# The projection's stores issued on GpSimd's queue instead of SyncE's, in a one-core diffusion-transformer layer

## The chip, the cores and the metric

The kernel runs on one core of one Trainium2 chip. Its time is device microseconds of one execution; the figure shown is the median of several executions. One profiled execution of the same program gives the trace: for every instruction its engine, its start and its length, and for every idle stretch what ended it. Five engines work side by side, each through its own list of instructions, strictly in order: PE multiplies matrices, DVE (VectorE) and ACT (ScalarE) do elementwise work, POOL (GpSimd) too, and SP (SyncE) only issues transfers. A transfer is issued from the list of some engine and then runs on 16 shared DMA engines; an instruction in a list that has to wait for something holds up everything behind it in that list.

## The reference

One layer over 2048 latent tokens and 256 context tokens, width 1024, all in float32.

```python
h     = modulate(x, norm1_g, shift, scale)       # RMSNorm, then (1 + scale) and shift
p     = h @ w_in        # columns: k | v | q | u | vg | gate_attn | gate_gmlp
...
q, k  = rmsnorm(q, q_norm_g), rmsnorm(k, k_norm_g)   # then rotary on both
attn  = attend(q, all latent and context k, v)
gm    = u * (W_s @ norm(vg) + b)                     # in chunks of 128 tokens
y     = sigmoid(gate_attn) * (attn @ w_br_attn) + sigmoid(gate_gmlp) * (gm @ w_br_gm)
x     = x + g1 * (y @ w_out)
x     = x + g2 * (square(relu(modulate(x, norm2_g, ...) @ w_ff1)) @ w_ff2)
```

That is the mathematics in short; heads, blocks and the context's own key and value columns are left out.

## The kernel before

**Stages.** The program runs the projection (until about 750 us), attention, the two branches' merge, and the feed-forward part. Every float32 operand is split into a high and a low half, and every product is three matmuls (L1705, L1706, L1707 for the wide ones; L185 to L187 for small ones). Latent tokens come in four blocks of 512 and are projected in two pairs of blocks. The 1792 columns ahead of the gates form two "pairs" (index 0: keys, values and queries, two halves of 384 columns; index 1: `u` and `vg`, two of 512), and the 2048 gate columns are cut into eight `Gate`s of two times 128 columns, for each pair of blocks. For both, a scheme of Strassen's kind is used: 7 products instead of 8, over sums and differences of the two blocks' halves and of the weights' halves. So the projection's elementwise work has to make weight combinations, operand halves and sums of products, besides the splits.

**What the projection stores.** Six places write intermediate tiles to HBM, where a later step loads them again:

- L556 in `h_ahead`: the second pair of blocks' normalized tokens, turned (16 stores of 256 KB into `h_d`).
- L628 in `opening_terms` and L677 in `terms`: the weights' combinations of pair 0 (16 of 192 KB) and pair 1 (16 of 256 KB), into `t_d`. `pair_chunk` loads them again at L701, ACT splits off the high half at L703 and DVE the low half at L704; then PE can use them. `terms` takes its four tiles of a round from the `m` buffers, of which there are four: two are loaded with weights (L663) and two hold the results (L670 to L673) until the four stores at L677 have landed.
- L2086 in `Pair.leave`: the sums of products of the pairs (64 stores into `pr_d`, shown as `p_d` in the profile). Half of them are issued by ACT, which has just copied them; the other half, which DVE adds up at L2084, by SP.
- L2103 in `Gate.store`: the gates' tanh (64 of 256 KB into `ta_d` and `tb_d`). ACT makes it at L2130 after DVE's sum (L2144 for product 4, L2149 for product 2), or straight from PSUM.
- L825 in `keys_work`: the finished keys (10 stores into `k_d`). Their making starts with statistics over the heads (L771) and ends with DVE's low half at L812 and PE's transposes at L191.

**What sets the order.** The projection is written as interleaved generators: a product's steps (`pairs_run`, `Gate.step`) call `tick`, which advances the queued work (`keys_work`, `queries_work`, `mixing`). Within the projection the compiler's scheduler then places each instruction on its engine's list by its own model of when it would be ready; only some loads, and the walls between stages, are pinned by hand. From attention on, the lists of PE and DVE are fixed by hand. Hence a change of a store's queue can move other instructions on any engine in the projection. The scheduler also hands out completion semaphores: transfers of SP and ACT share eight in turn, those of POOL have eight of their own, and a transfer waits until the one eight places earlier in that turn has landed.

**Buffers.** `t2` has six buffers of 2 KB a partition, `t4` eight of 4 KB, `m` four of 4 KB. A store that lands later keeps its buffer longer.

**POOL** has no work in the projection besides a few constants at the start; its sums for the modulation (L2299) begin when attention does.

Of the kernel before, what the change touches and what calls it, by code (L numbers as in the profile page):

```python
# [18 lines left out]
P = 128  # L19
# [25 lines left out]
HK = KC // 2  # L45
# [5 lines left out]
def f32(ap):  # L51
    return ap.bitcast(F32)
# [19 lines left out]
class Kern:  # L72
# [474 lines left out]
    def h_ahead(self, blk):  # L547
        for i in range(2):
            xs = self.x_load(self.x_block(2 * blk + i), TT, self.m4)
            yield  # L550
            self.h_scale(xs)
            yield
            for k in range(KC):
                ot = self.t2([TB])
                self.turn(xs, k, ot)
                self.nc.sync.dma_start(self.h_d[i][k % HK][:, k // HK], ot)  # L556
                yield

    def operand(self, p, src):
# [36 lines left out]
    def opening_terms(self, pair, direct):  # L596
        nc = self.nc
        tt, sub = nc.vector.tensor_tensor, ALU.subtract
        n, w = pair.n, self.I["w_in"][0]
        b, t = {}, {}  # L600
        for kk in range(HK):
            for k in (kk, kk + HK):
                r = [self.h2([n]) for _ in range(2)]
                for j in range(2):
                    lo = pair.lo + j * n
                    nc.sync.dma_start(r[j], w[k * P : (k + 1) * P, lo : lo + n])
                b[k] = [r[j] for j in pair.cols]
        yield

        def term(p, kk, in0, in1):  # L610
            t[p, kk] = self.sb("hx", [n])
            tt(out=t[p, kk], in0=in0, in1=in1, op=sub)

        def first(kk):
            term(4, kk, b[kk][1], b[kk][0])
            term(5, kk, b[kk + HK][1], t[4, kk])

        def split(p, c):
            hi, lo = self.f4([2, n], F32R), self.f4([2, n], F32R)
            direct.append([(hi[:, s], lo[:, s]) for s in range(2)])  # L620
            for s in range(2):
                nc.scalar.copy(hi[:, s], t[p, 2 * c + s])
            for s in range(2):
                tt(out=lo[:, s], in0=t[p, 2 * c + s], in1=f32(hi[:, s]), op=sub)

        def store(p):
            for kk in range(HK):
                nc.sync.dma_start(self.t_d[pair.index][p][kk // 2][kk % 2], t[p, kk])  # L628

        first(0)  # L630
        yield
        first(1)
        yield
        split(5, 0)
        yield
        first(2)
        first(3)
        yield
        split(5, 1)
        yield  # L640
        for kk in range(HK):
            term(6, kk, b[kk + HK][1], b[kk][1])
        for c in range(2):
            split(6, c)
        store(4)
        yield
        for kk in range(HK):
            term(3, kk, b[kk + HK][0], t[5, kk])
        store(3)
        yield  # L650
        store(6)
        store(5)
        yield

    def terms(self, pair, alloc):
        nc = self.nc
        tt, sub = nc.vector.tensor_tensor, ALU.subtract
        n, w = pair.n, self.I["w_in"][0]
        for kk in range(HK):
            rows = []  # L660
            for k in (kk, kk + HK):
                r = alloc([2, n])
                nc.sync.dma_start(  # L663
                    r.rearrange("p j c -> p (j c)"),
                    w[k * P : (k + 1) * P, pair.lo : pair.lo + 2 * n],
                )
                rows.append([r[:, j] for j in pair.cols])
            (b11, b12), (b21, b22) = rows
            t12, t34 = alloc([2, n]), alloc([2, n])
            tt(out=t12[:, 0], in0=b12, in1=b11, op=sub)  # L670
            tt(out=t12[:, 1], in0=b22, in1=t12[:, 0], op=sub)
            tt(out=t34[:, 0], in0=b22, in1=b12, op=sub)
            tt(out=t34[:, 1], in0=b21, in1=t12[:, 1], op=sub)  # L673
            for p, src in (
                (4, t12[:, 0]), (5, t12[:, 1]), (6, t34[:, 0]), (3, t34[:, 1]),
            ):
                nc.sync.dma_start(self.t_d[pair.index][p][kk // 2][kk % 2], src)  # L677
            yield

    def pair_load(self, pair, p, c):  # L680
# [109 lines left out]
    def keys_work(self, nt, b, kraw=None):  # L790
        nc = self.nc
        c = 0 if b is None else b + 1
        if b is not None:
            kraw = self.t2([TT, NKV, HD])
            nc.sync.dma_start(
                kraw.rearrange("p t h d -> p t (h d)"), self.rows(self.pr_d[0][b][0], slice(0, P))
            )
            yield
            yield
        (rb,) = self.heads_rstd([kraw[:, :nt]], 1.0 / HD)  # L800
        nc.vector.tensor_tensor(out=kraw[:, :nt], in0=kraw[:, :nt], in1=rb, op=ALU.mult)
        yield
        kr = self.t2([TT, NKV, HD])
        if b is None:
            g = self.rg["k"].unsqueeze(1).unsqueeze(1).broadcast_to([P, nt, NKV, HD])
            nc.vector.tensor_tensor(out=kr[:, :nt], in0=kraw[:, :nt], in1=g, op=ALU.mult)
        else:
            self.rope(self.rope_tables("k", b), kraw, kr, self.t2([TT, NKV, HD]), NKV)
        yield
        kk = self.m4([TT, NKV, 2, HD], F32R)  # L810
        nc.scalar.copy(kk[:, :nt, :, 0, :], kr[:, :nt])
        nc.vector.tensor_tensor(  # L812
            out=kk[:, :nt, :, 1, :], in0=kr[:, :nt], in1=f32(kk[:, :nt, :, 0, :]),
            op=ALU.subtract,
        )
        yield
        n = nt * P
        for kv in range(NKV):
            ps = self.bank([TB])
            self.transposes(  # L820
                ps, [f32(kk[:, t, kv]).rearrange("p a d -> p (a d)") for t in range(nt)]
            )
            ka = self.t2([TB])
            nc.scalar.copy(ka[:, :n], ps[:, :n])
            nc.sync.dma_start(self.k_d[c][kv][:, :n], ka[:, :n])  # L825
        yield

    def queries_work(self, b):
# [246 lines left out]
    def project(self, tail):  # L1075
# [9 lines left out]
        direct = []  # L1085
        terms = self.opening_terms(pairs[0], direct)
        next(terms)
        self.loads.append(range(at, self.here()))
        h[0], h[1] = [], []
# [9 lines left out]
        def opening(raw=raw, h=h):  # L1099
# [6 lines left out]
            for c in range(2):  # L1106
                for kk in (2 * c, 2 * c + 1):
                    t = raw[0, kk]
                    self.turn(self.x0, kk + HK, t[:, 1])
                    h[1].append(self.operand(1, t[:, 1]))  # L1110
                ready.append(self.pair_chunk(pairs[0], 1, c, loaded[2 + c]))
                next(terms)
            yield
            turned = self.raw_turned(1, x1, raw, self.t4)
            next(turned)
            next(terms)
            yield
            next(turned)
# [707 lines left out]
    def ff2(self, blk, side):  # L1826
# [60 lines left out]
        def take(p, t):  # L1887
            ps = banks[p][t]
            if p in (0, 5, 6):
                u = u3 if p == 6 else u2  # L1890
                u[t] = self.sb("f2", [TB])
                nc.scalar.copy(u[t], ps)
            else:
                leave(p, t, ps)
                if p == 1:
                    nc.scalar.copy(ps, u2[t])
# [159 lines left out]
class Pair:  # L2056
# [21 lines left out]
    def leave(self, i, j, t, ps, u=None):  # L2078
        k, nc = self.k, self.nc
        x = k.t2([TB])[:, : self.n]  # L2080
        if u is None:
            nc.scalar.copy(x, ps)
        else:
            nc.vector.tensor_tensor(out=x, in0=u, in1=ps, op=ALU.add)  # L2084
        dst = k.pr_d[self.index][2 * self.blk + i][j]
        (nc.scalar if u is None else nc.sync).dma_start(dst[t * P : (t + 1) * P, :], x)  # L2086


class Gate:
# [9 lines left out]
    def store(self, i, j, src):  # L2099
        k = self.k  # L2100
        dst = (k.ta_d, k.tb_d)[self.g // HK][2 * self.blk + i]
        lo = (2 * (self.g % HK) + j) * P
        self.nc.sync.dma_start(dst[lo : lo + P, :], src)  # L2103

    def last_weights(self, load):
        k, nc = self.k, self.nc
# [285 lines left out]
```

## Time and profile before

| what | value |
| --- | --- |
| median of three executions | 3017.25 us (3015.89, 3017.25, 3019.2) |
| profiled execution: whole / span of instructions | 3021.28 / 3019.5 us |
| granted TensorE clock, mean of the span | 0.989 |
| PE busy | 2942.4 us (97%) |
| DVE / ACT / POOL busy | 2091.8 / 1429.2 / 652.7 us |
| transfers | 537.02 MB in 385503 packets |
| reading of HBM / writing | 370.32 / 164.10 MB |

A row of a timeline gives the start, the length, the engine, the line of the program, the operation, and the tiles written and read (numbers of buffers left out); the bracket at the end says how long the engine sat idle before it and what ended that. A row of the view of waits adds up such idle time by what was waited for: engine, line, what released it, then microseconds in all, the number of times, and the longest. `SPq` is SP's list of transfers. The granted clock is the share of full speed that the chip's throttle gave TensorE.

### The profile page before, as it was taken

How to read it: one execution, taken by the hardware profiler on the slowest of the kernel's cores; microseconds unless marked ns; L12 is line 12 of the kernel's file. 1: busy time of each engine (PE TensorE's matmuls, PEld its weight loads, DVE VectorE, ACT ScalarE, POOL GpSimd, SP SyncE). 2: the span in 40 equal slices, each digit the busy share in tenths (PEclk: the TensorE clock that was granted, in tenths of full speed). 3: DMA queues.
4: the chain of work that ended last, by engine and by line, in shares of the span. 5: the costliest groups of instructions: out<-in, count | busy, mean ns of one | idle time of the engine just before them, and what ended most of it. 6: DMA issues, size and time to landing. Idle time of an engine off the chain costs nothing.

```text
span 3019.5 us, 37930 instructions
## 1 busy us (share of the span) xinstructions
PE 2942.4 (97%) x13325; PEld 2216.2 (73%) x13325; DVE 2091.8 (69%) x3019; ACT 1429.2 (47%) x2330; POOL 652.7 (22%) x470
## 2 busy tenths in 40 slices
PE   7899999999999999999999989999999999999999
PEld 5778788875555555555888878888887888888887
DVE  5857577885788888777655588776676766654555
ACT  5545765563455454544222254444454344444432
POOL 0000000000899899985212200000000000000000
PEclk9999999999999999999999999999999999999999
DMA  7586666554000010005766559888766544447554
GB/s 275 183 292 204 209 212 212 194 174 147 28 29 29 29 35 23 19 22 180 248 208 213 170 190 317 306 303 299 264 229 223 186 154 153 151 152 279 209 208 154
DMA packets 385503, 537.02 MB, mean 178 GB/s; under 512 B 37968, under 2 KB 197888, under 8 KB 385312
## 3 DMA queue, kind: packets, MB, share of 16 engines
q1 hardware_dynamic: 372944, 513.87, 51.5%
q10 hardware_dynamic: 12368, 20.73, 1.8%
q8 instruction: 105, 1.72, 0.2%
q14 instruction: 86, 0.70, 0.1%
HBM read 370.32 MB, written 164.10 MB: 177 GB/s over the span
## 4 chain that ended last, share of the span: by engine, by line
PE 84%; DVE 6%; DMA 5%; ACT 3%; issue 2%; SPq 0%; POOL 0%; ACTq 0%; DVEq 0%; POOLq 0%
PE b L1705 14%; PE b L1706 14%; PE b L1707 14%; PE b L2279 9%; PE b L2248 5%; PE b L2267 4%; PE b L185 4%; PE b L186 4%; PE b L187 4%; PE b L2203 3%; PE a L1705 3%; PE a L1706 3%; PE a L1707 3%; PE b L191 1%; DMA m<-in_w_in 1%
## 5 line engine op out<-in xcount | busy, mean ns | idle before, releaser
L2214 DVE TENSOR_REDUCE ts<-b 128x1 f32<-128x512 f32 x512 | 313.2, 683 | 74.7 <-PE b L2203 74.7
L2299 POOL TENSOR_TENSOR ac<-ac,p 128x512 f32<-128x512 f32 x214 | 306.4, 1463 | 51.6 <-ACT p L2271 51.6
L1821 DVE TENSOR_TENSOR b<-b,b 128x1024 fp32r<-128x1024 f32 x170 | 200.8, 1221 | 135.4 <-ACT b L1820 135.1
L1820 ACT CAST b<-b 128x1024 fp32r<-128x1024 f32 x170 | 170.6, 1050 | 223.8 <-PE b L1707 98.8
L2271 ACT ACTIVATE p<-b 128x512 f32<-128x512 f32 x384 | 194.1, 627 | 169.6 <-PE b L2267 168.9
L1706 PE MATMUL b<-b,b 128*128 128x512 f32 x680 | 265.2, 390 | 3.3 <-DVE b L1821 3.3
L1705 PE MATMUL b<-b,b 128*128 128x512 f32 x680 | 266.1, 391 | 1.7 <-DVE f L1842 1.5
L1707 PE MATMUL b<-b,b 128*128 128x512 f32 x680 | 264.7, 389 | 0.0
L2299 POOL TENSOR_TENSOR ac<-p,p 128x512 f32<-128x512 f32 x32 | 52.5, 1658 | 757.1 <-DMA raw<-in_w_mod 752.5
L2299 POOL TENSOR_TENSOR ac<-ac,t 128x512 f32<-128x512 f32 x152 | 204.9, 1376 | 0.0
L2248 PE MATMUL b<-h,h 128*128 128x512 f32 x576 | 189.2, 409 | 3.6 <-ACT p L2271 2.0
L2279 PE MATMUL b<-p,h 128*64 128x512 f32 x768 | 186.4, 608 | 0.0
L2267 PE MATMUL b<-h,h 128*128 128x512 f32 x576 | 179.8, 393 | 0.0
L1706 PE MATMUL b<-hb,b 128*128 128x512 f32 x446 | 173.8, 390 | 0.0
L1715 DVE TENSOR_TENSOR f<-f,b 128x512 f32<-128x512 f32 x160 | 109.3, 683 | 80.3 <-issue 46.6
L1705 PE MATMUL b<-hb,b 128*128 128x512 f32 x415 | 161.8, 390 | 0.0
L1707 PE MATMUL b<-hb,b 128*128 128x512 f32 x415 | 161.2, 389 | 0.0
L2248 PEld LDWEIGHTS b<-h,h 128*128 128x128 f32 x576 | 104.7, 190 | 65.0 <-DVE ts L2214 25.9
L1706 PEld LDWEIGHTS b<-b,b 128*128 128x128 f32 x680 | 127.7, 188 | 31.8 <-DVE b L1821 5.2
L1705 PEld LDWEIGHTS b<-b,b 128*128 128x128 f32 x680 | 127.6, 188 | 29.7 <-ACT b L1820 2.3
L1707 PEld LDWEIGHTS b<-b,b 128*128 128x128 f32 x680 | 127.7, 188 | 26.4
L1718 ACT ACTIVATE f<-f 128x512 f32<-128x512 f32 x96 | 60.5, 630 | 140.8 <-DVE f L1715 140.8
(434 smaller groups left out, 7290.7 us busy)
## 6 DMA issues: line engine op xcount, KB each, us to landing
ao_d<-f SPq DMA_DIRECT2D x224, 256.0 KB
f<-in_w_ff SPq DMA_DIRECT2D x48, 1024.0 KB
b<-ao_d SPq DMA_DIRECT2D x85, 512.0 KB
b<-w2o_d SPq DMA_DIRECT2D x85, 512.0 KB
w2o_d<-f SPq DMA_DIRECT2D x112, 256.0 KB
f<-in_w_in SPq DMA_DIRECT2D x44, 512.0 KB
f<-x_d SPq DMA_DIRECT2D x64, 256.0 KB
hb<-ao_d SPq DMA_DIRECT2D x54, 256.0 KB
```

What stands on the lines that cost most here:

```text
L185: mm(ps, sh, mh, start=start, stop=False)
L1705: mm(ps, wh, hh, start=start and k == 0, stop=False, skip_group_check=True)
L1706: mm(ps, wh, hl, start=False, stop=False, skip_group_check=True)
L1707: mm(ps, wl, hh, start=False, stop=k == len(w) - 1, skip_group_check=True)
L1820: nc.scalar.copy(h, f32(l))
L1821: nc.vector.tensor_tensor(out=l, in0=f32(l), in1=f32(h), op=ALU.subtract)
L2214: nc.vector.tensor_reduce(out=self.mx[:, t, h, c : c + 1], in_=ps[h], axis=AX.X, op=ALU.max)
L2248: self.nc.tensor.matmul(self.pts[j][h], k.KA[c][self.kv][:, ks], self.qa[h], start=True, stop=False, skip_group_check=True,)
L2267: self.nc.tensor.matmul(s, k.KB[c][self.kv][:, ks], self.qb[h], start=False, stop=True, skip_group_check=True,)
L2271: self.nc.scalar.activation(pt[h], s, AF.Exp)
L2279: nc.tensor.matmul(self.o[h * HD : (h + 1) * HD, :], k.V[c][:, i, self.kv * HD : (self.kv + 1) * HD], pt[h], start=j == 0, stop=j == NKT - 1,)
L2299: nc.gpsimd.tensor_tensor(out=self.acc[e][:, h], in0=old[:, h], in1=pt[h], op=ALU.add)
```

## The change

In six places, `nc.sync.dma_start` becomes `nc.gpsimd.dma_start`. What is stored, from where and to where stays the same. ACT's half of the stores of `Pair.leave`, and all loads, stay where they are.

```diff
 h_ahead
-                self.nc.sync.dma_start(self.h_d[i][k % HK][:, k // HK], ot)
+                self.nc.gpsimd.dma_start(self.h_d[i][k % HK][:, k // HK], ot)
...
 opening_terms
-                nc.sync.dma_start(self.t_d[pair.index][p][kk // 2][kk % 2], t[p, kk])
+                nc.gpsimd.dma_start(self.t_d[pair.index][p][kk // 2][kk % 2], t[p, kk])
...
 terms
-                nc.sync.dma_start(self.t_d[pair.index][p][kk // 2][kk % 2], src)
+                nc.gpsimd.dma_start(self.t_d[pair.index][p][kk // 2][kk % 2], src)
...
 keys_work
-            nc.sync.dma_start(self.k_d[c][kv][:, :n], ka[:, :n])
+            nc.gpsimd.dma_start(self.k_d[c][kv][:, :n], ka[:, :n])
...
 Pair.leave
-        (nc.scalar if u is None else nc.sync).dma_start(dst[t * P : (t + 1) * P, :], x)
+        (nc.scalar if u is None else nc.gpsimd).dma_start(dst[t * P : (t + 1) * P, :], x)
...
 Gate.store
-        self.nc.sync.dma_start(dst[lo : lo + P, :], src)
+        self.nc.gpsimd.dma_start(dst[lo : lo + P, :], src)
```

POOL's list grows from 276 rows to 430, SP's shrinks by the same 154. The compiler's scheduler moves other instructions with them. Three pieces of the difference between the two programs' lists follow: a row with a minus stands there before, one with a plus now, one without either in both.

On SP, the rounds in which `terms` makes pair 1's weight combinations beside the first two gates (`ta_d` are the gates' stores, `t_d` the combinations', `m` the weights, `f4` and `e2` other loads):

```order
-L2103 DMA ta_d1_107<-t4_312_1629 128x512
 L663 DMA m_354_1845<-in_w_in 128x1024
 L663 DMA m_355_1847<-in_w_in 128x1024
-L2103 DMA ta_d0_106<-t4_349_1825 128x512
 L685 DMA f4_385_2011<-in_w_in 128x2x512
-L677 DMA t_d512_4_0_177<-m_356_1849 128x512
-L677 DMA t_d512_5_0_179<-m_356_1849 128x512
-L677 DMA t_d512_6_0_181<-m_357_1850 128x512
-L677 DMA t_d512_3_0_175<-m_357_1850 128x512
-L2103 DMA ta_d0_106<-t4_307_1582 128x512
 L663 DMA m_361_1881<-in_w_in 128x1024
 L663 DMA m_362_1883<-in_w_in 128x1024
```

The stores between the rounds' loads have gone to POOL's list, and the loads of the second round follow those of the first with one load between them.

On DVE, the same rounds (the rows of L670 to L673 are a round each; `t4_349` and `t4_342` are a gate's sums, whose products lie in the PSUM bank `b_341`):

```order
 L672 TENSOR_TENSOR m_364_1886<-m_362_1883,m_361_1881 128x512
 L673 TENSOR_TENSOR m_364_1886<-m_362_1883,m_363_1885 128x512
-L2144 TENSOR_TENSOR t4_349_1825<-t4_342_1773,b_341_1760 128x512
-L704 TENSOR_TENSOR f4_395_2082<-f4_394_2080,f4_396_2083 128x1024
-L2149 TENSOR_TENSOR t4_342_1773<-t4_342_1773,b_341_1760 128x512
 L670 TENSOR_TENSOR m_368_1914<-m_366_1910 128x512
 L671 TENSOR_TENSOR m_368_1914<-m_367_1912,m_368_1914 128x512
 L672 TENSOR_TENSOR m_369_1915<-m_367_1912,m_366_1910 128x512
 L673 TENSOR_TENSOR m_369_1915<-m_367_1912,m_368_1914 128x512
-L704 TENSOR_TENSOR f4_408_2141<-f4_408_2141,f4_409_2143 128x1024
+L2144 TENSOR_TENSOR t4_349_1825<-t4_342_1773,b_341_1760 128x512
+L704 TENSOR_TENSOR f4_395_2082<-f4_394_2080,f4_396_2083 128x1024
 L670 TENSOR_TENSOR m_372_1942<-m_370_1938 128x512
+L2149 TENSOR_TENSOR t4_342_1773<-t4_342_1773,b_341_1760 128x512
```

The gate's two sums have moved from ahead of the third round to behind it, the second of them behind the first row of the fourth round too.

On PE, around a small product of the mixing (`b_680`, whose input was loaded shortly before) between wide products of gates (`b_662`):

```order
 L1706 MATMUL b_662_3620<-h_195_1028,f4_654_3574 128x512
 L1707 MATMUL b_662_3620<-h_194_1027,f4_655_3575 128x512
-L1705 MATMUL b_662_3620<-h_196_1031,f4_654_3574 128x512
-L1706 MATMUL b_662_3620<-h_197_1032,f4_654_3574 128x512
-L1707 MATMUL b_662_3620<-h_196_1031,f4_655_3575 128x512
-L1705 MATMUL b_662_3620<-h_198_1035,f4_654_3574 128x512
-L1706 MATMUL b_662_3620<-h_199_1036,f4_654_3574 128x512
-L1707 MATMUL b_662_3620<-h_198_1035,f4_655_3575 128x512
 L185 MATMUL b_680_3715<-m_677_3709,m_679_3713 128x256
 L186 MATMUL b_680_3715<-m_678_3710,m_679_3713 128x256
```

The small product stands six wide matmuls earlier than before.

## The prediction

> **What bounds the kernel now.** I began with the page's busy times and its chain of waits.
>
> ```profile
> PE 2942.4 (97%) x13325; PEld 2216.2 (73%) x13325; DVE 2091.8 (69%) x3019; ACT 1429.2 (47%) x2330; POOL 652.7 (22%) x470
> PE 84%; DVE 6%; DMA 5%; ACT 3%; issue 2%; SPq 0%; POOL 0%; ACTq 0%; DVEq 0%; POOLq 0%
> ```
>
> PE is idle for 77 us of a span of 3019.5, so no scheduling change can bring more than a few tens of microseconds. All 154 moved stores lie in the projection, so next came the windows of 50 us there (columns: elapsed, busy of PE, PEld, DVE, ACT, POOL, then the granted clock, the transfers' share, GB/s).
>
> ```profile
> 50.00:100.00 50.00, 45.65 (x242) 42.47 (x243) 43.12 (x75) 35.00 (x65) 0.00 (x0) 0.93 0.52 169
> 100.00:150.00 50.00, 41.93 (x220) 36.46 (x219) 39.64 (x90) 27.34 (x45) 0.00 (x0) 0.90 0.59 181
> 150.00:200.00 50.00, 45.81 (x204) 36.65 (x203) 28.30 (x49) 19.03 (x32) 0.00 (x0) 0.98 0.86 289
> 200.00:250.00 50.00, 49.51 (x230) 40.44 (x229) 36.08 (x67) 24.21 (x36) 0.00 (x0) 0.99 0.75 248
> 650.00:700.00 50.00, 41.40 (x183) 32.61 (x182) 31.19 (x53) 24.96 (x39) 0.00 (x0) 0.90 0.51 161
> ```
>
> PE's idle time is 4.35, 8.07, 4.19, 0.49 and 8.60 us in these; the two windows with the most also have the lowest clock, 0.90. The transfers are at 0.86 of their engines only from 150 to 200. POOL is empty. What PE waits for between 45 and 750 us, and what SP's list waits for up to 840 us, came last:
>
> ```profile
> PE a L1705 <- ACT a L2150: 8.3, 3, 5.1
> PE b L990 <- ACT m L519: 6.3, 2, 5.7
> PE b L185 <- DMA m<-ws_d: 4.4, 5, 2.4
> PE b L191 <- DVE m L812: 2.9, 1, 2.9
> SPq L2103 <- ACT t L2130: 148.8, 44, 11.3
> SPq L2086 <- DVE t L2084: 43.2, 25, 6.4
> SPq L556 <- ACT t L528: 24.1, 14, 8.7
> SPq L628 <- DVE hx L612: 23.4, 12, 10.0
> ACT f L703 <- DMA f<-t_d: 33.6, 11, 8.3
> ```
>
> SP spends 239.5 us (the four SP rows) at the head of its list on a store whose data isn't ready, with loads behind it. That is a lot, but no store is waited for by PE: PE waits for ACT and DVE. A load that comes earlier counts only where one of these four kinds of wait ends with it.
>
> **What the change removes.** SP's waits above, and the issues:
>
> ```profile
> L677 SPq DMA_DIRECT2D t_d<-m x16: 319/320/423, 159.0 to 192.1; - x16
> ```
>
> A store's issue has a median of 320 ns; 154 of them are 49 us of SP's list over 700 us. None of it is on the chain (SPq 0%), so by itself it is worth nothing. In sentences apart: the Trainium skill's page "DMA: Bandwidth & Descriptors", section "Issuing engines are not separate DMA queues", says that issuing from several engines saves only the sequencer's time, usually little beside the transfer. By that rule alone the sum would be zero; the waits of 239.5 us are the larger saving here, and no run yet shows what they are worth.
>
> **What it adds on POOL.** The trace has no transfer issued by POOL. The nearest rows bound it: SP's 0.32 us below, POOL's own work on such a tile above.
>
> ```profile
> L2299 POOL TENSOR_TENSOR ac<-ac,p 128x512 f32<-128x512 f32 x214 | 306.4, 1463 | 51.6 <-ACT p L2271 51.6
> POOL ac L2299 <- DMA raw<-in_w_mod: 752.5, 1, 752.5
> L2103 SPq DMA_DIRECT2D tb_d<-m x8: 319/322/338, 698.7 to 743.1; - x8
> ```
>
> 154 times 0.32 to 1.46 us is 49 to 225 us, inside the 752.5 us in which POOL has nothing to do, and I take zero for it. If that cover were gone, the last stores of the gates (up to 743.1) would hold back L2299, which has slack until the feed-forward part; a few microseconds at most. What counts is a later landing: a store that lands 1 us later keeps its `m` buffer 1 us longer. In `terms`, a round's results need the buffers of the round before, whose stores are issued 5 us or more ahead of the next L670 (rows below), so up to about 4 us later landing is hidden.
>
> **Where a load comes earlier: the context keys.** The longest gap of PE up to 600 us, and what stands before it, from the timelines of PE, ACT and SP:
>
> ```profile
> 111.00 0.47 PE L990 MATMUL b<-ident,m 128*128 128x128 f32 x1 [5.70 <-ACT m L519]
> 106.64 0.83 ACT L703 CAST f<-f 128x768 fp32r<-128x768 f32 x1 [6.24 <-DMA f<-t_d]
> 96.71 2.25 SPq L2086 DMA_DIRECT2D p_d<-t  x2
> 99.49 1.04 SPq L701 DMA_DIRECT2D f<-t_d  x1
> ```
>
> ACT sat 6.24 us for weights whose load SP issued at 99.49, behind two sums' stores that took it from 96.71 to 98.96. Without these the load goes out some 2.5 us earlier, and L519, PE's releaser, could follow: a gain of up to 2.5 us. But in the new lists ACT has two further splits (`f4_273`, `f4_282`; 0.83 us each by the row above) ahead of L519, and DVE their low halves. That gives some 1.7 us back. I take a gain of 1, with ends of −1 and 5.7 (the whole gap).
>
> **Where the new order costs: pair 1's weight combinations.** Rows of DVE, SP and PE:
>
> ```profile
> 169.90 0.69 DVE L670 TENSOR_TENSOR m<-m 128x512 f32<-128x512 f32 x1 [3.85 <-DMA m<-in_w_in]
> 172.89 0.68 DVE L2144 TENSOR_TENSOR t<-t,b 128x512 f32<-128x512 f32 x1
> 176.70 0.69 DVE L2149 TENSOR_TENSOR t<-t,b 128x512 f32<-128x512 f32 x1 [1.43 <-PE b L1707]
> 182.09 0.68 DVE L673 TENSOR_TENSOR m<-m,m 128x512 f32<-128x512 f32 x1
> 188.68 0.69 DVE L670 TENSOR_TENSOR m<-m 128x512 f32<-128x512 f32 x1 [3.57 <-DMA m<-in_w_in]
> 158.97 4.18 SPq L677 DMA_DIRECT2D t_d<-m  x4
> 163.77 1.22 SPq L663 DMA_DIRECT2D m<-in_w_in  x2
> 173.07 0.39 PE L1706 MATMUL a<-f,h 128*128 128x512 f32 x1
> 173.30 0.39 PE L1707 MATMUL a<-f,h 128*128 128x512 f32 x1
> 173.63 0.50 PE L1705 MATMUL b<-hx,e 128*128 128x512 f32 x1
> 179.22 0.39 PE L1705 MATMUL b<-hx,t 128*128 128x512 f32 x1
> 197.22 0.63 PE L191 MATMUL b<-ident,m 128*128 128x128 f32 x4 [2.88 <-DVE m L812]
> ```
>
> Each round of DVE waits for its weights, about 6 us after their issue (163.77 to 169.90) at 0.86 of the transfer engines, which the change doesn't speed up. In the old list the gate's sum L2144 ran at 172.89, before the third round, and PE's product into the same bank began at 173.63, on its heels. Now L2144 stands behind the third round, which ended at 182.09 + 0.68 = 182.77. The stores gone from SP's list bring that round forward: the second round's loads by some 1.5 to 2 us (they no longer follow the four L677 and a gate's store), the third by about 3 in all. So L2144 runs from 182.8 − 3 = 179.8 to 180.5. PE reaches its product 0.7 us later than before (three wide matmuls, at 0.23 us from start to start as at 173.07 and 173.30, are put ahead of it), at 174.3, and waits 180.5 − 174.3 = 6.2 us. If the transfers pull ahead by 5 us this is 4; by nothing, 9.
>
> L2149 then stands behind the first row of the fourth round, at 188.68 − 4 + 0.69 = 185.4, done by 186.1, and ACT's copy follows; PE wants the bank again at 179.22 + 6.2 = 185.4: another 1.5 us with a copy of some 0.6. On the other side, the key transposes at 197.22 stand 12 or more matmuls earlier but their input comes 4 us earlier too, and PE is 7.7 late: that gap of 2.88 goes. Net loss 6.2 + 1.5 − 2.9 = 4.8, ends 2 and 8.
>
> To this the clock answers: windows with a gap above 5 us ran at 0.90, the one here at 0.98. Falling to 0.90 for one such window is 0.08 of its 45.81 us of matmuls, 3.7 us; I take 3, ends 0 and 4.
>
> **Two small products.** These wait for a load that DVE's L156 releases, not a store:
>
> ```profile
> 384.79 0.36 PE L185 MATMUL b<-m,m 128*128 128x256 f32 x1 [2.44 <-DMA m<-ws_d]
> 627.71 0.39 PE L185 MATMUL b<-m,m 128*128 128x256 f32 x1 [0.74 <-DMA m<-ws_d]
> ```
>
> They now stand six and four wide matmuls earlier, each 0.23 us or more of cover gone: 1.4 + 0.9 = 2.3 us, I take 2, ends 0 and 4. Other waits (L2150's 8.3 us after 640) hang on DVE's order, which has no row of a store in it; zero, ends −4 and 4.
>
> **Sum.** −1 + 4.8 + 3 + 2 = +8.8 us, on the profiled 3021.28 (span 3019.5 and 1.78 around it), which was 4.03 above the median 3017.25. On the median: 3026.
>
> **The rivals.** *Faster: the late loads were what fed the gaps.* ACT's 33.6 us for `f<-t_d` and the stores' 239.5 us speak for it: if loads run far ahead, the rounds of `terms` come forward by 5 us or more and L2144 costs PE 4 instead of 6.2, the gap at 111.00 falls by most of its 5.7, and half of the 8.3 us behind L2150 goes with fuller buffers, with a clock of 0.93 instead of 0.90 in one window (0.03 × 42, 1.3 us): 4 + 1.5 − 2.9 + 2 − 5 − 4.2 − 1.3 = −6, and −11 if the rounds come so early that L2144 and L2149 cost nothing: 3006 to 3011, about 3008. Against it: PE's own waits name ACT and DVE.
>
> *No change.* The reordered sums cost 3 to 5 us, and the earlier loads and the vanished 2.88 give as much back; the clock stays. 3017 to 3021.
>
> *Slower by late landings.* If POOL writes descriptors slowly, `terms` decides: four stores at 3 us (twice POOL's row of 1463 ns) make 12 us in a round of 9.4 (169.90 to 188.68 are two rounds). Results wait for their buffers, each of three rounds slips by 3 us, PE stalls 9 more: 3035. It decides from about 2.4 us for a store. In sentences apart: the Trainium skill's "SBUF — State Buffer", section "SBUF: two separate sides", warns that a GpSimd transfer cannot write its descriptors while DVE runs a two-port operation, 620 ns becoming 3100. By that figure this rival is the forecast; here DVE's rows in these rounds are two-input sums (0.69 us for 512 elements), no copies, and no run yet shows whether they block it.
>
> *It does not do what it says.* All 16 engines are shared, and at 0.86 the loads land when they land: then the order alone acts, L2144 at 182.8, PE's stall 9: 3029, inside the forecast's range.
>
> **How the numbers follow.** Forecast (slower, 3020 to 3032) 0.40; faster 0.28; no change 0.17; late landings 0.15. About 0.2%, 6 us, is what a measurement of this kernel can tell from no change. Of the forecast 0.36 lies above 3023.3, and of its remainder 0.04 goes to no change: slower 0.36 + 0.15 = 0.51, same 0.21, faster 0.28. The range takes the faster case to its lower end, 3006, and late landings to 3 us beyond theirs, 3038; the forecast's own is 3020 to 3032.
>
> **What would show it.** In the changed profile: SP's rows of L2103, L2086, L677 gone; PE with a gap of 4 to 9 us before a product into a gate's bank near 174 us, ended by DVE's L2144, and no gap before L191 near 197; L185's gap near 385 above 2.44; a clock near 0.9 in that window; the gap near 111 smaller or the same. I am wrong if the L2144 gap is under 2 us, if gaps elsewhere shrink by more than 8 us in all, or if L670 and L672 wait for stores.

## The result, and the profile after

The changed kernel takes 3035.6 us (median of 4, 3035.51 to 3037.34), the one before 3018.22 (median of 4 in the end, 3015.89 to 3023.86): a ratio of 1.0056, 95% interval 1.0044 to 1.0068. It is slower by 17.4 us: the way that was forecast, and twice the 8.8. The time lies outside the 3020 to 3032 that the forecast gave for itself, and inside the 3006 to 3038 that takes in the rivals.

The page of the changed kernel: busy times and the chain that ended last.

```profile
PE 2942.5 (97%) x13325; PEld 2216.4 (73%) x13325; DVE 2091.0 (69%) x3019; ACT 1429.5 (47%) x2330; POOL 735.9 (24%) x624
PE 79%; issue 11%; DVE 3%; DMA 3%; ACT 2%; POOL 2%; SPq 0%; POOLq 0%; ACTq 0%; DVEq 0%
```

PE works as long as before (2942.5 us against 2942.4), in a span of 3035.6 instead of 3019.5. So the 16.1 us are all idle time of PE. POOL's rows rise from 470 to 624, by the 154 stores. Some windows of 50 us (columns as in the prediction):

```profile
100.00:150.00 50.00, 39.92 (x206) 34.59 (x205) 39.21 (x86) 27.98 (x45) 3.78 (x7) 0.86 0.50 156
150.00:200.00 50.00, 39.42 (x165) 31.04 (x163) 27.40 (x48) 16.85 (x28) 12.45 (x23) 0.92 0.85 291
300.00:350.00 50.00, 44.32 (x204) 35.46 (x203) 17.22 (x35) 35.21 (x55) 8.65 (x16) 0.95 0.66 219
```

From 150 to 200 us PE lost 6.4 us more than before (39.42 against 45.81), at a clock of 0.92 instead of 0.98; and a place that the prediction does not speak of, 300 to 350, lost 4.4 (44.32 against 48.73). PE's waits between 45 and 770 us, by what they waited for:

```profile
PE a L1705 <- ACT a L2150: 12.5, 4, 5.7
PE b L990 <- ACT m L519: 8.0, 2, 7.4
PE b L185 <- DMA m<-ws_d: 5.7, 6, 1.9
PE b L191 <- DVE m L812: 4.8, 1, 4.8
PE b L1705 <- ACT b L2150: 2.7, 1, 2.7
PE b L1705 <- DVE t L2144: 2.6, 2, 2.5
```

To see where the time goes, I took the start of the same-numbered matmul (of 13325) in each profile and subtracted that of the kernel before. The lists are reordered by a few dozen rows at most, so this is a lag, good to a microsecond or two:

| matmul (us in the kernel before) | changed | E1 | E2 | E5 | E7 | E8 | E11 | E12 |
| --- | --- | --- | --- | --- | --- | --- | --- | --- |
| 420 (104.3) | -2.5 | -2.1 | -1.4 | 0.0 | 0.8 | -0.8 | -2.1 | -2.0 |
| 480 (124.4) | 0.2 | -2.7 | 3.0 | 1.9 | 2.4 | -1.2 | 0.4 | -2.8 |
| 840 (205.0) | 9.6 | -4.0 | 10.6 | 15.9 | 2.3 | 9.8 | 1.6 | -2.1 |
| 960 (231.3) | 8.7 | -3.8 | 9.7 | 15.0 | 8.1 | 9.7 | 1.5 | -2.1 |
| 1200 (285.1) | 8.0 | -3.8 | 9.5 | 14.3 | 9.1 | 9.2 | 1.1 | -2.6 |
| 1440 (335.3) | 16.0 | 6.3 | 12.5 | 22.1 | 17.3 | 17.4 | 9.2 | 5.5 |
| 2280 (507.7) | 17.4 | 1.8 | 12.1 | 20.7 | 16.9 | 13.3 | 10.1 | 3.6 |
| 3400 (781.8) | 14.2 | -3.2 | 12.6 | 21.6 | 14.8 | 9.2 | 7.1 | -0.4 |

(E1 to E12 are the runs below.) The changed kernel falls behind by some 3 us around 110 us, by 8 to 9 between 159 and 205, and by 8 between 285 and 335; from 510 to 782 us it wins back 3, and stands 15.8 behind at the end. By chance alone profiles of the same lists differ by up to 3 us in the first 60 us (E1 is 1.5 ahead there, E6 below 1.7 behind), so columns are compared by what they gain or lose on the way. Each column is one execution, and that of the kernel before (3021.28) was itself 3 to 4 us above its medians.

**Between 159 and 205 us**, the place of the forecast. DVE, with one row of ACT, three of PE and one of SP behind:

```profile
179.34 0.68 DVE L673 TENSOR_TENSOR m<-m,m 128x512 f32<-128x512 f32 x1
179.94 0.68 DVE L2144 TENSOR_TENSOR t<-t,b 128x512 f32<-128x512 f32 x1
184.10 0.69 DVE L670 TENSOR_TENSOR m<-m 128x512 f32<-128x512 f32 x1 [2.34 <-DMA m<-in_w_in]
185.31 0.69 DVE L2149 TENSOR_TENSOR t<-t,b 128x512 f32<-128x512 f32 x1 [0.52 <-PE b L1707]
189.75 0.69 DVE L671 TENSOR_TENSOR m<-m,m 128x512 f32<-128x512 f32 x1 [3.14 <-DMA m<-in_w_in]
190.96 0.69 DVE L673 TENSOR_TENSOR m<-m,m 128x512 f32<-128x512 f32 x1
193.29 1.23 DVE L704 TENSOR_TENSOR f<-f,f 128x1024 fp32r<-128x1024 f32 x1 [1.65 <-ACT f L703]
194.43 0.41 DVE L771 TENSOR_REDUCE ts<-m 128x4 f32<-128x256 f32 x1
198.61 0.42 DVE L812 TENSOR_TENSOR m<-t,m 128x256 fp32r<-128x256 f32 x1 [0.47 <-ACT m L811]
192.21 1.05 ACT L703 CAST f<-f 128x1024 fp32r<-128x1024 f32 x1 [4.96 <-DMA f<-t_d]
164.22 0.67 PE L1705 MATMUL b<-hx,t 128*128 128x512 f32 x1 [2.69 <-ACT b L2150]
180.67 0.50 PE L1705 MATMUL b<-hx,e 128*128 128x512 f32 x1 [2.46 <-DVE t L2144]
199.18 0.45 PE L191 MATMUL b<-ident,m 128*128 128x128 f32 x1 [4.80 <-DVE m L812]
179.45 0.93 SPq L663 DMA_DIRECT2D m<-in_w_in  x2
```

and of the kernel before, one row of PE, two of DVE and one of SP:

```profile
162.87 0.50 PE L1705 MATMUL b<-hx,t 128*128 128x512 f32 x1 [1.31 <-ACT b L2150]
191.38 0.68 DVE L673 TENSOR_TENSOR m<-m,m 128x512 f32<-128x512 f32 x1
191.98 0.41 DVE L771 TENSOR_REDUCE ts<-m 128x4 f32<-128x256 f32 x1
183.18 1.06 SPq L663 DMA_DIRECT2D m<-in_w_in  x2
```

L2144 runs behind the third round's L673, at 179.94, and PE's product begins when it ends. The fourth round's weights were asked for at 179.45 instead of 183.18, but the second of the two tiles was there only for L671 at 189.75, and the round ended 0.4 us earlier than before. The keys were still 2 us later: L812 ran at 198.61 instead of 196.65. Before, their statistics (L771) followed the round at once. Now a low half (L704), which ran at 183.88 before, stands between the two. It waited for ACT's split L703, and that for a load (L701) that SP issued at 180.48, behind the fourth round's weights, instead of at 175.24, ahead of them. PE's transposes of these keys, which stand 35 rows earlier in its list than before, waited 4.80 us.

**Between 300 and 350 us**, rows of ACT, PE, SP and POOL of the changed kernel:

```profile
344.79 1.04 ACT L1038 CAST t<-f 128x1024 fp32r<-128x1024 f32 x1 [3.76 <-DMA tb_d<-t]
346.38 0.80 PE L1705 MATMUL a<-hx,t 128*128 128x512 f32 x1 [3.28 <-ACT a L2150]
334.59 1.76 SPq L496 DMA_DIRECT2D m<-in_x  x4
336.16 0.55 POOL L556 DMA_DIRECT2D h_d<-t  x1 [2.65 <-ACT t L528]
336.76 0.54 POOL L2103 DMA_DIRECT2D tb_d<-t  x1
```

and of the kernel before, SP at the same place of the program:

```profile
324.44 0.33 SPq L496 DMA_DIRECT2D m<-in_x  x1
325.63 0.32 SPq L556 DMA_DIRECT2D h_d<-t  x1
326.15 0.32 SPq L2103 DMA_DIRECT2D tb_d<-t  x1
326.56 0.41 SPq L496 DMA_DIRECT2D m<-in_x  x1
328.21 0.32 SPq L2103 DMA_DIRECT2D tb_d<-t  x1
328.62 0.90 SPq L496 DMA_DIRECT2D m<-in_x  x2
```

ACT's L1038 needs a `t4` buffer from which a gate's store reads. Before, SP's list held three of the four 512 KB loads of `x` behind stores that were waiting for their data, so the store had only one such load ahead of it. Now all four go out at once, and the store is issued 2 us later, behind 2 MB. It took 7.9 us to land (336.76 to 344.69). ACT stood 3.76 us, PE 3.28, and the window from 340 to 350 us has a granted clock of 0.76.

### The profile page after: what moved, and what is told of

Its sections match the earlier page's. It is cut to its first block, busy times and chain, and to the rows that moved or that the text cites. A ratio compares the mean times of both kernels' runs of the same rounds, so it can differ in the third digit from the quotient of the medians.

```text
span 3035.6 us, 38038 instructions
## 1 busy us (share of the span) xinstructions
PE 2942.5 (97%) x13325; PEld 2216.4 (73%) x13325; DVE 2091.0 (69%) x3019; ACT 1429.5 (47%) x2330; POOL 735.9 (24%) x624
## 4 chain that ended last, share of the span: by engine, by line
PE 79%; issue 11%; DVE 3%; DMA 3%; ACT 2%; POOL 2%; SPq 0%; POOLq 0%; ACTq 0%; DVEq 0%
PE b L1705 14%; PE b L1707 14%; PE b L1706 14%; PE b L2279 9%; PE b L2248 4%; PE b L2267 4%; PE b L185 4%; PE b L186 4%; PE b L187 4%; PE b L2203 3%; PE a L1705 2%; PE a L1707 2%; PE a L1706 2%; PE b L191 1%; DMA m<-ws_d 1%
## 5 line engine op out<-in xcount | busy, mean ns | idle before, releaser
L2299 POOL TENSOR_TENSOR ac<-ac,t 128x512 f32<-128x512 f32 x152 | 205.0, 1378 | 0.0
L156 POOL TENSOR_TENSOR bw<-bw,bw 128x512 fp32r<-128x512 f32 x58 | 75.4, 1322 | 236.3 <-ACT bw L152 236.3
```

The source lines that it names most:

```text
L2299: nc.gpsimd.tensor_tensor(out=self.acc[e][:, h], in0=old[:, h], in1=pt[h], op=ALU.add)
```

## The experiments

To part the queue from the order, a table of the instructions' order holds the scheduler to a given one: every instruction, engine by engine, after the one that preceded it in that table.

```diff
+        pin(self, dep)
...
+def pin(kern, dep):
+    insts = list(kern.nc.cur_bb.bb.instructions)
+    tail = {}
+    for k in order_table():
+        i = insts[k]
+        if i.engine in tail:
+            kern.tc.add_manual_dep(i, tail[i.engine], dep, reason="order")
+        tail[i.engine] = i.name
```

With the kernel before's own table this gives back its lists row for row. All runs have such a table; what differs is the table and the queue.

**E1 and E2: queue and order, crossed.** E1 is the change with the table of the kernel before: PE, DVE and ACT read row for row as before, and 154 rows move from SP's list to POOL's. E2 is the kernel before with the changed kernel's table.

> The stores stand on POOL's queue as in the change, but PE, DVE, ACT and SP keep the order of the kernel before, row for row. Order theory (the loss of 17.4 us comes from the scheduler's new order of DVE's and ACT's rows): within 5 us of the kernel before, about 3019, and PE has no gap above 1.5 us before the product into the gate's bank near 174 us. Landing theory (stores issued on POOL land 3 to 9 us after their issue behind loads and hold the t4 and m buffers): the same loss under the old order, 3030 or more, with waits on the landing of ta_d, tb_d and t_d stores.

> All stores on SP's queue as before, but PE, DVE, ACT and the loads in the changed kernel's order, row for row. Order theory: as slow as the change, 3032 to 3038, since L2144 still stands behind the third round of the weight combinations. Landing theory: back at the kernel before, 3018 to 3022. A third case, that the new order is worse on SP's queue than on POOL's since the stores again stand ahead of loads: above 3038.

E1: 3021.73 us, ratio 1.0014 (1.0004 to 1.0024). E2: 3028.66, ratio 1.0035 (1.0021 to 1.0049). The order alone costs about 10.5 us, the queue alone about 4, which together is most of 17.4 and, within the intervals, all of it. The order is the larger cause, though E2 stays below the 3032 to 3038 that was expected of it. But E1 also shows the landing theory right at one place: it is level or ahead until 300 us and loses 10 us by 335, with ACT's wait of the kind seen above:

```profile
334.61 1.04 ACT L1038 CAST t<-f 128x1024 fp32r<-128x1024 f32 x1 [5.21 <-DMA tb_d<-t]
```

E2, on SP's queue, loses only 3 there. The 10 us aren't kept: by 782 us E1's profile has won 9.5 of them back (last row of the table), so the 4 us rest on its median and not on this profile. And E1 wins nothing to speak of before 300 us although its SP list has no store in it (E4 below, with all stores on SP, stands at -2.9 where E1 is at -4.0).

**E3 and E4: is it POOL's queue, or the loads' place ahead of the store?** E3 is E1 with the eight loads of `x` for the second pair's tokens on POOL too, between the stores. E4 is the kernel before, with nothing but this changed in SP's list:

```diff
 E3
-            xs = self.x_load(self.x_block(2 * blk + i), TT, self.m4)
+            xs = self.x_load(self.x_block(2 * blk + i), TT, self.m4, queue=self.nc.gpsimd)
...
 E4, rows of SP
 L496 DMA m_604_3302<-in_x
+L496 DMA m_605_3304<-in_x
+L496 DMA m_606_3306<-in_x
+L496 DMA m_607_3308<-in_x
 L556 DMA h_d0_3_148<-t2_599_3274
 L2103 DMA tb_d1_111<-t4_573_3112
-L496 DMA m_605_3304<-in_x
 L2103 DMA tb_d0_110<-t4_603_3298
-L496 DMA m_606_3306<-in_x
-L496 DMA m_607_3308<-in_x
```

> The stores on POOL and the old order of PE, DVE and ACT (as in the first run), and the eight loads of x for the second pair's tokens on POOL's queue too, between the stores where SP's list had them. If ACT's wait of 5.2 us near 334 us (L1038, for the landing of a tb_d store) comes from four such loads of 512 KB being issued ahead of the store, it shrinks below 1 us and the time falls by 4 to 7 us from the first run's 3021.7, to 3015 to 3018. If POOL's stores land late by themselves, the wait stays above 3 us and the time within 3 us of the first run's.

> The kernel before, all stores on SP, with one thing moved: three of the four loads of x near 324 us stand ahead of two tb_d stores and an h_d store in SP's list instead of between and behind them. If the loads' place ahead of the stores is what counts, the same wait of L1038 appears without POOL, 4 to 6 us, and the kernel is 4 to 7 us slower than before. If it is POOL's own queue, no change (within 2 us).

E4: 3022.07, ratio 1.0013 (1.0004 to 1.0022), 4 to 5 us slower. The wait appears without any transfer on POOL, on ACT:

```profile
332.23 1.04 ACT L1038 CAST t<-f 128x1024 fp32r<-128x1024 f32 x1 [4.77 <-DMA tb_d<-t]
```

So the wait comes from the place of the loads ahead of the store. All runs bear this out: before this row of ACT stand 3.6 to 5.2 us in the changed kernel, E1, E4, E5, E7, E8, E9, E11 and E12, where the four loads go out ahead of it, and at most 0.53 in the kernel before, E2, E3, E6 and E10. What the wait is worth in the end is less clear: E4's profile loses 5.8 us there and has them back by 782 us. E3: 3021.56, ratio 1.0016 (1.0004 to 1.0028): its time missed the expectation of 3015 to 3018, and is E1's. The wait of L1038 is gone, as expected, but the tokens come later, and PE waits for them a little further on (ACT, then PE):

```profile
331.20 1.05 ACT L1038 CAST t<-f 128x1024 fp32r<-128x1024 f32 x1 [0.53 <-DMA tb_d<-t]
345.15 1.01 PE L191 MATMUL b<-ident,m 128*128 128x128 f32 x4 [2.71 <-ACT m L519]
```

**E5: three rows of DVE back, alone.** The changed kernel, with this on DVE:

```diff
+L2144 TENSOR_TENSOR t4_349_1825
+L704 TENSOR_TENSOR f4_395_2082
+L2149 TENSOR_TENSOR t4_342_1773
 L670 TENSOR_TENSOR m_368_1914
...
-L2144 TENSOR_TENSOR t4_349_1825
-L704 TENSOR_TENSOR f4_395_2082
 L670 TENSOR_TENSOR m_372_1942
-L2149 TENSOR_TENSOR t4_342_1773
```

> The changed kernel with three rows of DVE put back: the gate's sums L2144 and L2149 and one low half (L704) stand ahead of the third round of the weight combinations again, everything else as changed. If these rows cost what the prediction says (7.7 us of stalls, 3 of clock), the progress of PE by 205 us against the kernel before falls from 8.5 us behind to 2 or less, and the time to 3027 to 3030. If the rounds are held by the transfers anyway and PE is late for another reason, no more than 2 us comes back.

A clear miss: 3041.58, ratio 1.0074 (1.0057 to 1.0091), slower than the change itself. DVE now waits for PE's products ahead of the rounds, so these end later, and PE's early transposes wait the longer. DVE and PE of E5:

```profile
178.81 0.69 DVE L2144 TENSOR_TENSOR t<-t,b 128x512 f32<-128x512 f32 x1 [6.48 <-PE b L1707]
183.88 0.69 DVE L2149 TENSOR_TENSOR t<-t,b 128x512 f32<-128x512 f32 x1 [3.25 <-PE b L1707]
203.69 0.42 DVE L812 TENSOR_TENSOR m<-t,m 128x256 fp32r<-128x256 f32 x1 [0.47 <-ACT m L811]
204.26 0.45 PE L191 MATMUL b<-ident,m 128*128 128x128 f32 x1 [11.35 <-DVE m L812]
```

The gate's rows are half of a trade: ahead of the round they hold the keys, behind it the gate. E5 leaves the transposes 35 rows early and the low half (L704) ahead of the keys' statistics; no run moves one of these two alone.

**E6: the gates' stores back on SP**, at their old places; the other 90 stores on POOL, the old order.

```diff
-        self.nc.gpsimd.dma_start(dst[lo : lo + P, :], src)
+        self.nc.sync.dma_start(dst[lo : lo + P, :], src)
```

> The old order, the four kinds of edit besides the gates' on POOL, the 64 gate stores back on SP at their old places among the loads. By the theory of loads running ahead of stores the wait of L1038 near 334 us is gone, since SP's list again issues these stores ahead of the loads, and the time is 3014 to 3018. By the theory that POOL's queue costs by its own slowness, what is left of it (90 stores of 154) costs half: 3019 to 3020.

3020.0, ratio 1.0008 (0.9998 to 1.0017). L1038 no longer waits for a landing (0.52 us before it, ended by issue, where E1 has 5.21), but 1.7 us against E1 cannot be told from nothing. Its time is above the 3014 to 3018 of the theory of loads ahead of stores and at the upper end of the other's 3019 to 3020, with an interval of 3 us either way: this run doesn't decide by its time.

**E7, E8, E9 and E11: the new order by regions.** A region is a stretch that has the same instructions in both orders, put back (or brought in) on PE, DVE, ACT and SP at once. C is that of the weight combinations (PE's matmuls 612 to 868, in the kernel before from 150 to 211 us; the other engines' rows begin some 15 us earlier), D the next (to 249 us, the other keys and queries), B the context keys (105 to 141 us); the expectations give these times roughly. In E7, E9 and E11 the changed kernel gets C, B, and C and D of the old order. E8 is E1 with C of the new one.

> The changed kernel with one region of its order put back on PE, DVE, ACT and SP together, the one in which pair 1's weight combinations are made and the context's keys are transposed (PE from about 137 to 220 us). If that region's order holds the larger part of the loss, PE is 1 to 3 us behind the kernel before at 205 us instead of 8.5 to 9.6, no gap above 3 us stands before L191 near 199, and the time falls from 3035.6 to 3027 to 3030. If the queue makes the loss there (stores and loads in each other's way), the lag at 205 us stays above 6.

> The stores on POOL, the old order everywhere (as in the first run) but in that one region, which has the changed kernel's order. If the region's order is the cause by itself: PE 5 to 8 us further behind at 205 us than in the first run, a gap of 3 to 5 us before L191 and one of 2 to 4 before the product that waits for L2144, and 3027 to 3030. If it costs only together with the other moved rows, within 3 us of the first run's 3021.7.

> The changed kernel with the order put back around the context keys instead (PE from about 100 to 135 us, with ACT's splits ahead of L519). Prediction's account of that place: the two splits and low halves ahead of L519 cost what the earlier load gains, so 2 to 3 us come back there (the gap before L990 falls from 7.4 to about 5.4), the rest stays: 3032 to 3034. If this place also sets off what follows (the rounds start earlier against the same transfers), nothing is left of it by 205 us: 3035 to 3036.

> The changed kernel with two neighbouring regions of its order put back together on PE, DVE, ACT and SP: the one of the weight combinations and the next, in which the other keys and queries are transposed (PE from about 137 to 245 us). The run before put back the first alone and lost 5.3 us at an L191 near 219 instead. If the later region's moved transposes were only hidden by the earlier loss, the lag at 245 us is now 1 to 3 us and the time 3027 to 3030. If the lag at 245 us stays above 6, the queue or the buffers make it, not the order.

E8: 3031.28, ratio 1.0039 (1.0026 to 1.0051): C's order by itself makes E1 slower by about 0.0025, 7.5 us; its time is a little above the 3027 to 3030 expected. From 159 to 205 us it loses 10 us where E1 gains 1.3, with the same wait before L191, while PE's wait for L2144 is only 0.9 us:

```profile
198.06 0.66 PE L191 MATMUL b<-ident,m 128*128 128x128 f32 x2 [4.71 <-DVE m L812]
```

E7 puts the same region back into the changed kernel and its time doesn't move: 3036.56, ratio 1.0064 (1.0051 to 1.0078). At 205 us it is 2.3 behind, as expected, and then it loses 5 to 6 us at the next transposes, which the new order also has earlier, and where the changed kernel, already late, doesn't wait. PE of E7:

```profile
219.31 0.98 PE L191 MATMUL b<-ident,m 128*128 128x128 f32 x6 [4.39 <-DVE m L812]
```

E11 puts both back: 1.5 behind at 231 us, 3027.98, ratio 1.0036 (1.0021 to 1.0051), 6 us back from 1.0056. So D's loss was hidden behind C's, and undoing one uncovers the other. E9 wins back what was expected at its place (L990's gap is 5.16 instead of 7.39) and nothing in the time: 3037.19, ratio 1.0060 (1.0047 to 1.0073). Its lag at 205 us is 7.0 instead of 9.6, and its profiled time, 3035.37, stands 2 us below that of the changed kernel; five runs from 3031.91 to 3039.65 don't show such a difference.

**E12: the old order up to the end of D, the new one behind.**

> The changed kernel with the old order up to about 245 us, the new one behind it. By the two runs above (old order alone on POOL's queue 3021.7; the rest of the new order behind 245 us, the two L185 groups among it, priced at 2 in the prediction): 3022 to 3026, with the 6 us wait of L1038 near 330 us still there. If the new order behind 245 us holds a loss of its own beyond that, above 3028.

3028.71, ratio 1.0030 (1.0020 to 1.0039), above the expected 3022 to 3026: the new order behind 245 us costs about 5 us more than E1's. Its profile doesn't show which rows: it fell on one of the shortest runs (3022.19, of 3020.65 to 3032.12) and ends 0.7 us behind the kernel before.

**E10: a faster version?** The kernel before, stores on SP, with the context keys' transposes 12 matmuls later on PE, and 12 wide products put ahead of the L185 of `b_680`.

> The kernel before, stores on SP, with two of PE's small groups put later: the context keys' transposes (L191) 12 matmuls later, and 12 wide matmuls ahead of the L185 of b_680, which waited 2.44 us. If such a wait is worth its full length: the gaps of 2.88 and 2.44 go, and the time is 3011 to 3014. If other waits grow in their place, within 2 us of the kernel before.

3019.53, ratio 1.0003 (0.9995 to 1.0012): no gain. It also shows that a table costs nothing that can be seen. Of the two waits, 0.31 us and none are left, and others stand a little behind them; the profile fell on one of the two shortest runs (3014.14). PE of E10:

```profile
217.89 0.30 PE L191 MATMUL b<-ident,m 128*128 128x128 f32 x1 [2.17 <-DVE m L812]
389.42 0.44 PE L1705 MATMUL a<-f,h 128*128 128x384 f32 x1 [2.51 <-ACT h L563]
```

No version beat the kernel before.

## Why the prediction was right, and where it was half

**The account.** By the ratios: the queue under the old order 0.0014 (E1), 4 us; the new order behind 245 us 0.0016 (E12 against E1), 5 us; the new order ahead of it 0.0026 (the change against E12), 8 us. The intervals leave each some 3 to 5 us either way. Of its +8.8 the forecast had 6.8 for the last (7.8 for the weight combinations, 1 off for the context keys), 2 for the one before it, at two products that turned out to cost nothing, and nothing for the queue.

**What was right, and what was luck.** That the new order costs, and that the earlier loads don't pay for it, was right, and so was the clock from 150 to 200 us (0.92 for "near 0.9"). Most of the other signs that the prediction named failed: the gap ended by L2144 is 2.46 us and not 4 to 9, the one before L191 grew instead of going, that before L185 near 385 shrank (below), and that near 111 grew from 5.70 to 7.39. "Under 2 us" at L2144, its own sign of being wrong, was missed by half a microsecond, and L672 did wait for a store once (0.93 us). The 3035 of the rival of late landings meets the measured 3035.6 by luck: it came from stores of 3 us each on POOL.

**SP's waits are worth nothing: right.** They were said to count only where one of PE's waits ends with them. E1 removes all of them and is not faster. This agrees with the rule of the Trainium skill that the prediction weighed ("DMA: Bandwidth & Descriptors", "Issuing engines are not separate DMA queues"), that other issuing engines save only the sequencer's time; what the rule does not tell is what those waits had done for the order of the transfers.

**POOL's price: right, the cover of landings wrong.** A store takes POOL 0.54 us, between the bounds of 0.32 and 1.46. The view of one line (L677, then L2103), with how long its stores took to land:

```profile
L677 POOL DMA_DIRECT2D t_d<-m x16: 539/539/548, 157.5 to 192.0; - x16
DMA to landing us min/median/max: 2.5/5.3/9.0
```

```profile
L2103 POOL DMA_DIRECT2D ta_d<-t x32: 539/539/556, 136.8 to 660.9; - x32
DMA to landing us min/median/max: 2.3/3.6/8.7
```

"Up to about 4 us later landing is hidden" was worked out for the `m` buffers, and there it held but for 0.93 us of DVE before an L672. It failed for the gates' `t4` buffers, which the step didn't look at. The rival of late landings had the right kind of event at the wrong place and by the wrong cause: not slow issues on POOL, but loads that no longer wait behind stores (E4).

**The context keys: the term had the wrong sign.** Gain 1, ends -1 and 5.7; measured a loss of 2.7 on the way from matmul 420 to 480, outside the ends. The load did come earlier: L703, which followed it at 106.64, ran at 101.24. But L519 waits for DVE's L178 as well, and that stood behind low halves moved ahead of it. "That gives some 1.7 us back" counted ACT's two splits and not DVE's rows. E1, with the old order, lost nothing there.

**The weight combinations: the sum right by luck, its parts not.** Predicted 4.8 for the stalls and 3 for the clock, 7.8; the lag grows by 8.5 from matmul 660 to 900, of which 6.4 are stalls by the windows. The times of DVE's rows came out within 0.6 us (L2144 at 179.94 for 179.8, the fourth round's L670 at 184.10 for 184.7). But PE, stalled 1.4 us more at 164.22 and slowed, reached the bank late, and waited 2.46 us for L2144 and not 6.2. And the step "that gap of 2.88 goes" failed: it grew to 4.80. It took the keys' input to come 4 us earlier as the fourth round's first row did, and the transposes to stand 12 or more matmuls earlier. They stand 35 earlier, some 8 us at 0.23 each, and the input came 2 us later: the round's second tile was there only 9.7 us after its issue, so that the rounds ended at 191.6 instead of 192.1, and L704 with its late load stood ahead of the keys' statistics. So 3.7 us too much for L2144 made up for 4.8 too little at L191. E5 and E8 say the same: without the wait for L2144, or with 0.9 us of it, the loss is as large or larger. The fourth round's late tile fits the rival "it does not do what it says", by which the loads land when the shared engines let them, though the third round did come 2.8 us earlier (L673 at 179.34 for 182.09); no run here took the stores' bytes away to show it.

**Two small products: no cost.** L185 waited 1.94 us instead of 2.44 and 0.30 instead of 0.74, although it stands earlier; the 2 us were wrong. The gap near 385 varies from run to run by more than the change: 1.2 to 3.1 us in the six runs with the old order there (E10 apart), 0.9 to 2.6 in the seven with the new one. The row L185 as a whole grew by 1.3 us (5.7 for 4.4), at other places.

**Other waits: zero, ends -4 and 4.** This is the term that was mis-sized most. Between 285 and 335 us the changed kernel loses 7.9, most of it at L1038 and at a clock of 0.76 around it; how much of that is kept to the end is open, since E1 and E4 win theirs back. It was left at zero because no store stood in the row that PE waited for; that a store's landing stood two steps further up (PE for L2150, L2150 behind L1038 on ACT, L1038 for the buffer) wasn't followed.

**What stays open:** which rows behind 245 us cost the 5 us of E12; which of C's rows (the gate's sums, L704 with its load, the transposes) costs what; and of E1's 4 us, how much is the wait at 334 us, since E3, without it, is as slow as E1, and E6, without it, lies within error of both E1 and the kernel before.

## What to carry to other kernels

A store that waits at the head of a list also paces the loads behind it: before moving it, count the bytes that can now be issued ahead of it, and ask which buffer its landing frees. Where a scheduler sets the order by its own model, a changed queue is a changed order; hold the order with a table to see the two apart. And a wait that is undone alone may only uncover the next (E5, E7, E10): put back a region on all engines at once before naming one row as the cause.

## What the runs showed of the hardware

POOL took 0.54 to 0.56 us for each store but the first (0.69), at 128, 192 and 256 KB alike: shortest and longest of L677's are 539 and 548 ns, and 124 of the 154 ran beside some instruction of DVE. The Trainium skill's "SBUF — State Buffer", section "SBUF: two separate sides", warns of descriptors held up by DVE; no issue here shows it beside DVE's two-input sums, and none fell beside a copy of DVE. From issue to landing it took 2.0 us at the shortest (L825, keys of 128 KB) and 9.0 at the longest (L677, at a transfer share of 0.97); E4 shows that loads ahead of a store are enough for a long one. And the granted clock fell at gaps of PE of 2 to 3 us, in windows of 10 us further than the 50 us windows of the prediction show. These three windows of the changed kernel go with gaps of 2.69, 2.46 and 3.28 us; in the kernel before, 160 to 170, 180 to 190 and 330 to 340 ran at 1.00, with no gap above 1.31:

```profile
160.00:170.00 10.00, 7.31 (x25) 5.57 (x24) 5.78 (x9) 3.16 (x5) 3.25 (x6) 0.83 1.02 374
180.00:190.00 10.00, 9.33 (x34) 7.52 (x35) 3.99 (x7) 2.41 (x4) 2.53 (x5) 0.83 0.97 329
340.00:350.00 10.00, 6.72 (x23) 5.11 (x22) 1.36 (x5) 6.19 (x11) 0.54 (x1) 0.76 0.89 291
```
